# Moving an expert's output turns, and the next expert's gather, to other places between the streamed weight steps

## The chip, the cores and the metric

The kernel runs on one core of one Trainium2 chip. The metric is the device time of one launch in microseconds; the time before is the median of three runs. The rows below come from one execution that the hardware profiler recorded. Engines are named as the profile names them: PE multiplies matrices (PEld is its weight loading), DVE and ACT work elementwise, POOL is a programmable engine, SP issues the weight transfers.

## The reference, cut to what matters

Two decoder layers over 256 tokens of width 1024, all in float32. Each layer adds a mixer and a feed-forward part; the feed-forward part of the second layer is a mixture of eight experts, of which each token takes two. Only this last part is touched:

```
def moe_swiglu(h, w_router, w_gate, w_up, w_down):
    top_vals, top_idx = lax.top_k(logits, 2)       # logits = h @ w_router
    gates = jax.nn.softmax(top_vals, axis=-1)
    ...
    y_e = (silu(x_e @ w_gate[e]) * (x_e @ w_up[e])) @ w_down[e]   # x_e: tokens of expert e
    out[token] += gate * y_e[token]
```

(The last two lines stand for the reference's sort into blocks.) w_gate[e] and w_up[e] are 1024 x 3584, w_down[e] is 3584 x 1024: 44.04 MB for an expert, 352 MB for the eight, read once each.

## The kernel before, in words

**Steps.** The experts' stage is a loop over `q` from 0 to 15. `q` is half of an expert: `e, h = divmod(q, 2)`, and a half is 1792 of the 3584 hidden columns. A `q` has a gate step (`mm_in("g", q, ...)`, L984), then the down step of the half before it (`mm_down(q - 1, ...)`, L1028), then its up step (`mm_in("u", q, ...)`, L984). Called gate 5, down 4, up 5 below. `silu` (L1004, ACT) and `hidden` (L1016 and L1017, DVE) make the hidden values from the gate's and the up step's sums.

**Tokens.** An expert has room for 96 tokens in three tiles of 32. Where it has 64 or fewer, PE branches over the third tile (the `If` of `third`, branch rows L994 and L1040).

**The ring of weights.** `Stream` loads weights in the order in which the steps use them, through SP, into nine slots (`RING_A` 4 and `RING_B` 5). Of a step's weights there are four transfers: 4 x 1792 KB for a gate or up step, 2 x 2048 and 2 x 1536 KB for a down step, so 7.34 MB for any step. A slot is released when PE has read it in the first or the second half of its step (`ws.done`), and the transfer nine places later in the order is then issued (L189).

**An expert's small work.** Between the streamed steps PE does four small things for each expert:

- `fetch(e)` (L966): 16 matmuls with a one-hot matrix `G` gather the expert's tokens from `hn` into `xe`; two PSUM banks, emptied by ACT and DVE (L968).
- `prepare(e)` (L320 and L1065): transposes the one-hot matrix into `S`, and the tokens' gates into `gs`.
- `y_turn(e, n)` for n = 0, 1 (L320): four transposes each turn the expert's output `yt` back; ACT (L1083) and DVE (L1084) write it, times the gate, as two parts into `y`. `yt` comes from `y_evac` after the expert's second down step.
- `scatter(e, t, v)`, four times (L1090): two matmuls each spread `y` over the tokens, and DVE adds the result to `xt` (L1092).

All four take their PSUM from `bank("C")`, which has two banks that are handed out in turn: what comes next on a bank waits until ACT and DVE have read what stood there.

**What sets the order.** PE and SP run in the order in which the program is written (`manual_schedule`); ACT's and DVE's order is set by the framework's scheduler. Before, the small work stands at two places: `y_turn` of expert e-1 and `fetch` of expert e+1 behind up step 2e, and `scatter` of e-1 and `prepare` of e behind gate step 2e+1.

Of the kernel before, what the change touches and what calls it, by code (L numbers as in the profile page):

```python
# [20 lines left out]
E = 8  # L21
# [19 lines left out]
def hybrid_decoder(  # L41
# [20 lines left out]
    def bank(tag):  # L62
        return psum.tile([P, 512], F32, tag=tag, name=f"ps{tag}", bufs=NB[tag])
# [255 lines left out]
    def tp(dst, src, n=P):  # L319
        PE.matmul(dst, lhsT=src, rhs=ident[:n, :n], start=True, stop=True, is_transpose=True)  # L320
# [590 lines left out]
    def onehot(scol, base, tag, scale=None):  # L911
        n = base.shape[-1]
        g = moe.tile([P, 2, n], F32, tag=tag, name=tag, bufs=1)
        for t in range(2):
            if scale is None:
                DVE.tensor_scalar(g[:, t], base, scol(t), None, op0=OP.is_equal)
            else:
                DVE.tensor_scalar(g[:, t], base, scol(t), scale(t), op0=OP.is_equal, op1=OP.mult)
        return g
# [6 lines left out]
    def gates():  # L926
        r = r_ffn
        DVE.tensor_copy(gr[:, :, :, 1], r[:, :, None].to_broadcast([P, 2, E]))
        m = [sm2("m1"), sm2("m2")]
        mv = sm2("mv")  # L930
        v12 = sm(4, "v12").rearrange("p (n t) -> p n t", n=2)
        for n in range(2):
            DVE.tensor_scalar(m[n], rk, float(n), None, op0=OP.is_equal)
            DVE.tensor_tensor(mv, m[n], lg, op=OP.mult)
            DVE.tensor_reduce(v12[:, n], mv, op=OP.add, axis=AX.X)
        dv = sm(2, "dv")
        DVE.tensor_tensor(dv, v12[:, 1], v12[:, 0], op=OP.subtract)
        DVE.tensor_tensor(dv, dv, r, op=OP.mult)
        g2 = sm(2, "g2")
        ACT.activation(g2, dv, AF.Exp)  # L940
        g1 = sm(2, "g1")
        DVE.tensor_scalar(g1, g2, 1.0, None, op0=OP.add)
        DVE.reciprocal(g1, g1)
        DVE.tensor_tensor(g2, g2, g1, op=OP.mult)
        for n, g in enumerate((g1, g2)):
            DVE.tensor_tensor(m[n], m[n], g[:, :, None].to_broadcast([P, 2, E]), op=OP.mult)
        DVE.tensor_tensor(gr[:, :, :, 0], m[0], m[1], op=OP.add)
        ps = bank("C")
        PE.matmul(ps[:, 0:8], lhsT=ones, rhs=sel[:, 0], start=True, stop=False)
        PE.matmul(ps[:, 0:8], lhsT=ones, rhs=sel[:, 1], start=False, stop=True)  # L950
        cnt = sm(1, "cnt")
        DVE.tensor_reduce(cnt, ps[:, 0:8], op=OP.max, axis=AX.X)
        DVE.tensor_copy(cnt_i, cnt)
        DVE.tensor_copy(cnt_e, ps[:, 0:8])


    def fetch(e):

        g = onehot(lambda t: slot[:, t, e:e + 1], io, "G0", lambda t: r_ffn[:, t:t + 1])
        xe = moe.tile([P, KD, CAP], F32, tag="xe", name="xe")  # L960
        for n in range(2):
            ps = bank("C")[:, 0:4 * CAP].rearrange("p (j l) -> p j l", j=4)
            for j in range(4):
                c = 4 * n + j
                for t in range(2):
                    PE.matmul(ps[:, j], lhsT=hn[:, t, c * P:(c + 1) * P], rhs=g[:, t],  # L966
                              start=(j == 0 and t == 0), stop=(t == 1), skip_group_check=True)
            (DVE.tensor_copy if n else ACT.copy)(xe[:, 4 * n:4 * n + 4], ps)  # L968
        return dict(e=e, x=xe)
# [3 lines left out]
    def third(e):  # L973

        return tc.If(counts[e] > 64) if counts else ExitStack()

    def mm_in(nm, q, x):
        banks = [bank("A") for _ in range(3)]

        def tile_of(t, k0, n):  # L980
            for k in range(k0, k0 + n):
                raw = ws.direct(MU[nm, q, k - k % 2])
                for j in range(4):
                    PE.matmul(banks[t][32 * j:32 * j + 32, 0:LW], lhsT=x[:, k, 32 * t:32 * t + 32],  # L984
                              rhs=raw[:, k % 2, LW * j:LW * j + LW], start=(k == 0), stop=(k == KD - 1),
                              skip_group_check=True)

        for k0 in range(0, KD, 4):
            for k in (k0, k0 + 2):
                for t in range(2):  # L990
                    tile_of(t, k, 2)
                if k == 0:
                    tile_of(2, 0, 1)
            with third(q // 2):  # L994
                k = max(k0, 1)
                tile_of(2, k, k0 + 4 - k)
            for k in (k0, k0 + 2):
                ws.done(MU[nm, q, k])
        return banks

    def silu(bg):
        sg = big.tile([P, 3, LW], F32, tag="x0", name="sg")
        for t in range(3):
            ACT.activation(sg[:, t], bg[t][:, 0:LW], AF.Silu)  # L1004
        return sg
# [41 lines left out]
    def y_evac(psd):  # L1047

        yc = big.tile([P, 3, 256], F32, tag="x4", name="yc")
        yt = moe.tile([P, KD, CAP], F32, tag="yt", name="yt", bufs=1)  # L1050
        ACT.copy(yc[:, 0:2].rearrange("p t n -> p (t n)"), psd[0])
        ACT.copy(yc[:, 2], psd[1][:, 0:256])  # L1052
        for t in range(3):
            DVE.transpose(yt[:, :, 32 * t:32 * t + 32], yc[:, t].rearrange("p (n c) -> p n c", c=32))  # L1054
        return yt

    def prepare(st):

        e = st["e"]
        g = onehot(lambda t: slot[:, t, e:e + 1], io, "G1")  # L1060
        ps = bank("C")
        for t in range(2):
            tp(ps[0:CAP, t * P:(t + 1) * P], g[:, t])
        for t in range(2):
            PE.matmul(ps[0:CAP, T:T + 1], lhsT=g[:, t], rhs=gr[:, t, e, 0:1], start=(t == 0), stop=(t == 1),  # L1065
                      skip_group_check=True)
        s = moe.tile([P, T], F32R, tag="S", name="S", bufs=1)
        ACT.copy(s[0:CAP], ps[0:CAP, 0:T])
        gs = moe.tile([P, 1], F32, tag="gs", name="gs")
        DVE.tensor_copy(gs[0:CAP], ps[0:CAP, T:T + 1])  # L1070
        st["s"], st["gs"] = s, gs

    def y_turn(st, n):

        if n == 0:
            st["y"] = big.tile([P, 2, D], F32R, tag="x2", name="y")
        ps = bank("C")
        for b in range(4):
            tp(ps[0:CAP, b * P:(b + 1) * P], st["yt"][:, 4 * n + b])
        g = st["gs"][0:CAP]  # L1080
        q = slice(512 * n, 512 * n + 512)
        hi, lo = st["y"][0:CAP, 0, q], st["y"][0:CAP, 1, q]
        ACT.activation(hi, ps[0:CAP], AF.Copy, scale=g)  # L1083
        DVE.scalar_tensor_tensor(lo, ps[0:CAP], g, hi.bitcast(F32), op0=OP.mult, op1=OP.subtract)  # L1084

    def scatter(st, t, v):
        ps = bank("C")
        q = slice(512 * v, 512 * v + 512)
        for i in range(2):
            PE.matmul(ps, lhsT=st["s"][0:CAP, t * P:(t + 1) * P], rhs=st["y"][0:CAP, i, q],  # L1090
                      start=(i == 0), stop=(i == 1))
        DVE.tensor_tensor(xt[:, t, q], xt[:, t, q], ps, op=OP.add)  # L1092
# [3 lines left out]
    st = {0: fetch(0)}  # L1096
    psd = ht = None
    for q in range(NS):
        e, h = divmod(q, 2)
        bg = mm_in("g", q, st[e]["x"])  # L1100
        if q == 0:
            gates()
        sg = silu(bg)
        if h and e:
            for t in range(2):
                for v in range(2):
                    scatter(st[e - 1], t, v)
            st.pop(e - 1)
            prepare(st[e])
        if 0 < q < NS - 1:  # L1110
            if h:
                psd = [bank("B"), bank("B")]
            mm_down(q - 1, ht, psd)
            if not h:
                st[e - 1]["yt"] = y_evac(psd)
        bu = mm_in("u", q, st[e]["x"])
        hp, ht = ht, hidden(sg, bu, q == NS - 1)
        if h == 0:
            if e:
                for n in range(2):  # L1120
                    y_turn(st[e - 1], n)
            if e + 1 < E:
                st[e + 1] = fetch(e + 1)
            if e == 0:
                prepare(st[e])
        if q == 0:
            _, counts = nc.values_load_multi_w_load_instructions(
                cnt_e[0:1, 0:E], engines=[mybir.EngineType.PE], min_val=0, max_val=T,
                skip_runtime_bounds_check_because="a count of 256 tokens")
# [146 lines left out]
```

## Time and profile before

| | |
|---|---|
| median of three runs | 1343.11 us (1339.17 to 1346.61) |
| the profiled execution | 1340.84 us, of which the program's span is 1338.8 us |
| mean granted clock of PE | 0.984 of full speed |
| PE busy | 1224.2 us, 91% of the span |
| DVE, ACT busy | 460.2 us (34%), 267.1 us (20%) |
| HBM read | 420.74 MB, 315 GB/s over the span |

The span has two parts. Up to about 440 us run the mixers and the dense layer; from there to the end run the experts, with the router's last work at the seam. In the experts' part both the matrix engine and the transfers are busy nearly all the time, so that an average does not tell which of them sets the pace; stretches have to be looked at one by one. All times in rows are microseconds from the span's start unless marked ns.

### The profile page before, as it was taken

The numbers are of one execution on the slowest core, as the hardware profiler recorded it, in microseconds if no ns is written. First come the engines' busy times: TensorE is split into PE (matmuls) and PEld (weight loads), VectorE is DVE, ScalarE is ACT, GpSimd is POOL, SyncE is SP. The second block draws the span as 40 slices with busy tenths as digits, with TensorE's granted clock in tenths as the row PEclk, the third lists the DMA queues.
The fourth block names the chain that finished last, engine by engine and source line by source line (L and its number), as shares of the span: only waits on it lengthen the run. The fifth ranks groups of instructions, "written<-read, shape, count | busy, mean of one in ns | idle before, by whom it ended". The sixth has DMA issues, their size and how long they took to land. (4 is left out here: it accounts for less than half of the span.)

```text
span 1338.8 us, 28436 instructions
## 1 busy us (share of the span) xinstructions
PE 1224.2 (91%) x12994; PEld 775.1 (58%) x12994; DVE 460.2 (34%) x927; ACT 267.1 (20%) x446; POOL 11.9 (1%) x25
## 2 busy tenths in 40 slices
PE   4999999999999899999999999899897987887884
PEld 4997999999997644344444435434433523433342
DVE  3998765557897310102012010211211110210212
ACT  3671544445661200000000000100100000100001
POOL 3000000000000000000000000000000000000000
PEclk9999999999999899999999999999999999999997
DMA  8751565555340998998899699999999999999993
GB/s 171 277 189 63 173 237 184 174 178 175 140 173 28 381 405 338 412 410 320 361 397 416 263 423 420 407 417 416 421 421 417 422 420 416 423 419 418 419 388 135
DMA packets 91300, 423.98 MB, mean 317 GB/s; under 512 B 4590, under 2 KB 33493, under 8 KB 83476
## 3 DMA queue, kind: packets, MB, share of 16 engines
q1 hardware_dynamic: 90452, 421.09, 79.6%
q0 software_dynamic: 688, 0.72, 0.6%
q8 instruction: 122, 2.00, 0.6%
q14 instruction: 22, 0.18, 0.0%
q10 hardware_dynamic: 16, 0.00, 0.0%
HBM read 420.74 MB, written 1.05 MB: 315 GB/s over the span
## 5 line engine op out<-in xcount | busy, mean ns | idle before, releaser
L984 PE MATMUL psA<-raw,xe 128*32 128x448 f32 x5024 | 488.7, 541 | 30.2 <-DMA raw<-in_moe_w_up_dram 14.1
L984 PEld LDWEIGHTS psA<-raw,xe 128*32 128x32 f32 x5024 | 168.0, 110 | 337.5 <-issue 291.7
L1028 PE MATMUL psB<-raw,ht 128*32 128x256 f32 x4296 | 241.8, 380 | 20.3 <-DMA raw<-in_moe_w_down_dram 13.0
L1028 PEld LDWEIGHTS psB<-raw,ht 128*32 128x32 f32 x4296 | 143.3, 110 | 118.4 <-DMA raw<-in_moe_w_down_dram 23.4
L396 PE MATMUL psB<-xh,whi 128*128 128x256 f32 x608 | 173.1, 285 | 0.0
L398 PE MATMUL psB<-xh,wlo 128*128 128x256 f32 x608 | 172.5, 284 | 0.0
L397 PE MATMUL psB<-xl,whi 128*128 128x256 f32 x608 | 172.2, 283 | 0.0
L1016 DVE TENSOR_TENSOR pr<-psA,sg 128x448 f32<-128x448 f32 x48 | 43.0, 921 | 346.1 <-PE psA L984 297.3
L223 DVE TENSOR_TENSOR wlo<-raw,whi 128x1024 fp32r<-128x1024 f32 x110 | 134.2, 1224 | 59.7 <-ACT whi L222 59.6
L222 ACT CAST whi<-raw 128x1024 fp32r<-128x1024 f32 x110 | 115.0, 1050 | 113.9 <-PE psB L397 51.7
L1004 ACT ACTIVATE sg<-psA 128x448 f32<-128x448 f32 x48 | 24.5, 543 | 474.6 <-PE psA L984 464.6
L396 PEld LDWEIGHTS psB<-xh,whi 128*128 128x128 f32 x608 | 116.6, 192 | 0.7 <-issue 0.7
L397 PEld LDWEIGHTS psB<-xl,whi 128*128 128x128 f32 x608 | 116.5, 192 | 0.0
L398 PEld LDWEIGHTS psB<-xh,wlo 128*128 128x128 f32 x608 | 116.5, 192 | 0.1
L1054 DVE STREAM_TRANSPOSE yt<-yc 128x256 f32<-128x256 f32 x24 | 9.7, 431 | 245.4 <-ACT yc L1052 245.1
L680 PE MATMUL psA<-yf,raw 128*128 128x256 f32 x256 | 62.2, 399 | 5.4 <-ACT yf L720 3.0
L680 PEld LDWEIGHTS psA<-yf,raw 128*128 128x128 f32 x256 | 49.7, 199 | 13.5 <-ACT yf L720 3.5
L1092 DVE TENSOR_TENSOR xt<-xt,psC 128x512 f32<-128x512 f32 x32 | 20.8, 685 | 106.3 <-PE psC L1090 106.3
L966 PE MATMUL psC<-G,hn 128*128 128x96 f32 x256 | 36.1, 309 | 18.4 <-DVE y L1084 14.7
L527 DVE SCALAR_TENSOR_TENSOR conv<-gp,pc,conv 128x256 f32<-128x256 f32 x120 | 50.9, 480 | 0.0
L397 PE MATMUL psA<-al,whi 128*128 128x256 f32 x176 | 49.8, 283 | 0.0
L398 PE MATMUL psA<-ah,wlo 128*128 128x256 f32 x176 | 49.7, 282 | 0.0
(266 smaller groups left out, 874.5 us busy)
## 6 DMA issues: line engine op xcount, KB each, us to landing
raw<-in_moe_w_gate_dram SPq DMA_DIRECT2D x64, 1792.0 KB, 12.1
raw<-in_moe_w_up_dram SPq DMA_DIRECT2D x64, 1792.0 KB, 24.3
raw<-in_moe_w_down_dram SPq DMA_DIRECT2D x30, 2048.0 KB
raw<-in_moe_w_down_dram SPq DMA_DIRECT2D x30, 1536.0 KB, 17.6
raw<-in_w_in_dram SPq DMA_DIRECT2D x9, 2048.0 KB, 14.0
raw<-in_ffn_w_gate_dram SPq DMA_DIRECT2D x11, 1024.0 KB, 5.6
raw<-in_ffn_w_up_dram SPq DMA_DIRECT2D x11, 1024.0 KB, 8.1
raw<-in_ffn_w_down_dram SPq DMA_DIRECT2D x5, 2048.0 KB, 9.1
```

The costliest lines, as they stand in the source:

```text
L222: ACT.copy(hi, raw)
L223: DVE.tensor_tensor(lo, raw, hi.bitcast(F32), op=OP.subtract)
L396: PE.matmul(ps, lhsT=hi, rhs=xh, start=start, stop=False, **kw)
L397: PE.matmul(ps, lhsT=hi, rhs=xl, start=False, stop=False, **kw)
L398: PE.matmul(ps, lhsT=lo, rhs=xh, start=False, stop=stop, **kw)
L527: DVE.scalar_tensor_tensor(conv[:, c], src, w, conv[:, c], op0=OP.mult, op1=OP.add)
L680: PE.matmul(acc[j][:, a], lhsT=raw[:, k, w], rhs=yf[b][:, k], start=(b + k == 0 and a == 0), stop=(b + k == 4), skip_group_check=True)
L966: PE.matmul(ps[:, j], lhsT=hn[:, t, c * P:(c + 1) * P], rhs=g[:, t], start=(j == 0 and t == 0), stop=(t == 1), skip_group_check=True)
L984: PE.matmul(banks[t][32 * j:32 * j + 32, 0:LW], lhsT=x[:, k, 32 * t:32 * t + 32], rhs=raw[:, k % 2, LW * j:LW * j + LW], start=(k == 0), s ...
L1004: ACT.activation(sg[:, t], bg[t][:, 0:LW], AF.Silu)
L1016: DVE.tensor_tensor(pr[:, t], by(bu[t][:, 0:LW]), by(sg[:, t]), op=OP.mult)
L1028: PE.matmul(psd[t // 2][32 * j:32 * j + 32, 256 * (t % 2):256 * (t % 2) + 256], lhsT=ht[:, t, b], rhs=w[:, j], start=(h == 0 and b == 0 an ...
```

## The change

`y_turn` goes from behind up step 2e to behind gate step 2e+1, ahead of down step 2e. `fetch`, `scatter` and `prepare` go behind that down step, in this order, ahead of up step 2e+1. For q = 15, where no down step stands between gate and up, `y_turn`, `scatter` and `prepare` follow each other directly. `prepare(0)` and `fetch(1)` move from q = 0 to q = 1 in the same way. No instruction is added or removed.

```diff
         sg = silu(bg)
         if h and e:
-            for t in range(2):
-                for v in range(2):
-                    scatter(st[e - 1], t, v)
-            st.pop(e - 1)
-            prepare(st[e])
+            for n in range(2):
+                y_turn(st[e - 1], n)
         if 0 < q < NS - 1:
             if h:
                 psd = [bank("B"), bank("B")]
             mm_down(q - 1, ht, psd)
             if not h:
                 st[e - 1]["yt"] = y_evac(psd)
+        if h:
+            if e + 1 < E:
+                st[e + 1] = fetch(e + 1)
+            if e:
+                for t in range(2):
+                    for v in range(2):
+                        scatter(st[e - 1], t, v)
+                st.pop(e - 1)
+            prepare(st[e])
         bu = mm_in("u", q, st[e]["x"])
         hp, ht = ht, hidden(sg, bu, q == NS - 1)
-        if h == 0:
-            if e:
-                for n in range(2):
-                    y_turn(st[e - 1], n)
-            if e + 1 < E:
-                st[e + 1] = fetch(e + 1)
-            if e == 0:
-                prepare(st[e])
```

PE's order around the second turn (`y_turn` of expert 1; `G_6890` is the one-hot matrix of the gather for expert 3, `G_7043` that of `prepare(2)`), before:

```order
L320 MATMUL psC<-ident,yt 96x128 x8
L966 MATMUL psC<-G_6890,hn 128x96 x16
L984 MATMUL psA<-raw,xe 32x448 x36
L994 COMPARE_AND_BRANCH
L984 MATMUL psA<-raw,xe 32x448 x12
L994 UNCONDITIONAL_BRANCH x2
L984 MATMUL psA<-raw,xe 32x448 x32
L994 COMPARE_AND_BRANCH
L984 MATMUL psA<-raw,xe 32x448 x16
L994 UNCONDITIONAL_BRANCH x2
L1090 MATMUL psC<-y,S 128x512 x8
L320 MATMUL psC<-ident,G_7043 96x128 x2
```

The same place after (`G_7183` and `G_7223` are the same two matrices under other numbers):

```order
L320 MATMUL psC<-ident,yt 96x128 x8
L1028 MATMUL psB<-raw,ht 32x256 x68
L1040 COMPARE_AND_BRANCH
L1028 MATMUL psB<-raw,ht 32x256 x28
L1040 UNCONDITIONAL_BRANCH x2
L1028 MATMUL psB<-raw,ht 32x256 x48
L1040 COMPARE_AND_BRANCH
L1028 MATMUL psB<-raw,ht 32x256 x24
L1040 UNCONDITIONAL_BRANCH x2
L966 MATMUL psC<-G_7183,hn 128x96 x16
L1090 MATMUL psC<-y,S 128x512 x8
L320 MATMUL psC<-ident,G_7223 96x128 x2
```

Between the transposes and the next use of the C banks there now stands a whole down step, and gather, scatter and `prepare` follow each other without a streamed step between them.

DVE's order at this place, before:

```order
L1016 TENSOR_TENSOR pr<-psA,sg 128x448 x2
L1017 STREAM_TRANSPOSE ht<-pr 128x448 x2
L1084 SCALAR_TENSOR_TENSOR y<-psC,gs,y 96x512 x2
L968 COPY xe<-psC 128x384
L918 TENSOR_SCALAR G_7782<-io,slot,rstd 128x96 x2
L994 UNCONDITIONAL_BRANCH x2
L1092 TENSOR_TENSOR xt<-xt,psC 128x512 x4
L916 TENSOR_SCALAR G_7935<-io,slot 128x96 x2
L1070 COPY gs<-psC 96x1
```

And after:

```order
L1016 TENSOR_TENSOR pr<-psA,sg 128x448 x2
L1017 STREAM_TRANSPOSE ht<-pr 128x448 x2
L994 UNCONDITIONAL_BRANCH x2
L1084 SCALAR_TENSOR_TENSOR y<-psC,gs,y 96x512 x2
L1040 UNCONDITIONAL_BRANCH x2
L968 COPY xe<-psC 128x384
L1092 TENSOR_TENSOR xt<-xt,psC 128x512 x4
L918 TENSOR_SCALAR G_8075<-io,slot,rstd 128x96
L1070 COPY gs<-psC 96x1
L918 TENSOR_SCALAR G_8075<-io,slot,rstd 128x96
L916 TENSOR_SCALAR G_8115<-io,slot 128x96 x2
```

The two writes of `y` (L1084) stood directly behind the products and transposes of `hidden`, and now a gate step later; the four sums into `xt` (L1092) now stand directly behind the copy of the gathered tokens (L968).

PE's order at the last odd step, q = 15, before (then the rest of gate 15, and the scatter behind it):

```order
L320 MATMUL psC<-ident,yt 96x128 x8
L984 MATMUL psA<-raw,xe 32x448 x36
L994 COMPARE_AND_BRANCH
L984 MATMUL psA<-raw,xe 32x448 x12
L994 UNCONDITIONAL_BRANCH x2
```

And after:

```order
L320 MATMUL psC<-ident,yt 96x128 x8
L1090 MATMUL psC<-y,S 128x512 x8
L320 MATMUL psC<-ident,G_11482 96x128 x2
L1065 MATMUL psC<-gr,G_11482 96x1 x2
L984 MATMUL psA<-raw,xe 32x448 x36
```

Here nothing stands between the transposes and the scatter any more.

## Rows read from the trace of the kernel before

**Rows 1.** Who waited: PE's waits from 430 us on (total us, times, longest).

```profile
PE psC L966 <- DVE y L1084: 14.7, 6, 2.6
PE psA L984 <- DMA raw<-in_moe_w_up_dram: 14.1, 13, 2.3
PE psB L1028 <- DMA raw<-in_moe_w_down_dram: 13.0, 12, 1.7
PE psA L984 <- DMA raw<-in_moe_w_gate_dram: 11.1, 11, 1.7
```

**Rows 2.** Stretches: window, PE, PEld, DVE, ACT, POOL busy (instructions), PE clock, DMA share, GB/s.

```profile
620.00:660.00 40.00, 39.51 (x546) 18.92 (x542) 3.13 (x7) 1.89 (x4) 0.00 (x0) 1.00 0.79 309
...
740.00:770.00 30.00, 29.50 (x402) 14.07 (x398) 3.13 (x7) 1.89 (x4) 0.00 (x0) 1.00 0.72 275
770.00:840.00 70.00, 68.91 (x912) 33.09 (x904) 8.65 (x13) 3.18 (x7) 0.00 (x0) 1.00 1.02 421
840.00:880.00 40.00, 35.77 (x420) 19.31 (x421) 6.82 (x15) 2.83 (x6) 0.00 (x0) 0.96 0.99 404
880.00:1280.00 400.00, 347.90 (x4050) 154.77 (x4049) 59.96 (x101) 23.58 (x47) 0.00 (x0) 0.99 1.01 420
```

**Rows 3.** PE in order of time, around the first turn (start, us, what, idle before).

```profile
608.24 1.08 PE L320 MATMUL psC<-ident,yt 128*96 128x128 f32 x8
611.90 3.81 PE L966 MATMUL psC<-G,hn 128*128 128x96 f32 x32 [2.58 <-DVE y L1084]
615.64 18.25 PE L984 MATMUL psA<-raw,xe 128*32 128x448 f32 x192
633.82 1.20 PE L1090 MATMUL psC<-y,S 96*128 96x512 f32 x4
635.33 1.33 PE L1090 MATMUL psC<-y,S 96*128 96x512 f32 x4 [0.32 <-DVE xt L1092]
636.83 0.42 PE L320 MATMUL psC<-ident,G 128*96 128x128 f32 x2 [0.17 <-DVE xt L1092]
...
637.44 18.34 PE L1028 MATMUL psB<-raw,ht 128*32 128x256 f32 x336
```

**Rows 4.** DVE in order of time, at the first turn.

```profile
610.05 1.16 DVE L1017 STREAM_TRANSPOSE ht<-pr 128x448 f32<-128x448 f32 x2
611.14 1.36 DVE L1084 SCALAR_TENSOR_TENSOR y<-psC,gs,y 96x512 fp32r<-96x512 f32 x2
615.75 0.56 DVE L968 COPY xe<-psC 128x384 f32<-128x384 f32 x1 [3.25 <-PE psC L966]
```

**Rows 5.** PE in order of time, the gathers of the second and third turn.

```profile
731.62 3.81 PE L966 MATMUL psC<-G,hn 128*128 128x96 f32 x32 [2.58 <-DVE y L1084]
...
842.06 5.44 PE L966 MATMUL psC<-G,hn 128*128 128x96 f32 x32 [2.46 <-DVE y L1084]
```

**Rows 6.** The stretch of the third gather, columns as in rows 2.

```profile
842.00:847.50 5.50, 5.44 (x36) 5.35 (x40) 0.66 (x2) 0.48 (x1) 0.00 (x0) 0.69 0.99 417
```

**Rows 7.** SP's issues of weight transfers, four of them (start, us to the last one, what).

```profile
766.08 0.37 SPq L189 DMA_DIRECT2D raw<-in_moe_w_gate_dram  x1
...
800.47 0.89 SPq L189 DMA_DIRECT2D raw<-in_moe_w_up_dram  x2
...
854.55 0.89 SPq L189 DMA_DIRECT2D raw<-in_moe_w_up_dram  x2
...
872.28 6.37 SPq L189 DMA_DIRECT2D raw<-in_moe_w_gate_dram  x3
```

**Rows 8.** PE in order of time, the last down steps and the last turn.

```profile
1285.62 4.09 PE L1028 MATMUL psB<-raw,ht 128*32 128x256 f32 x72 [1.69 <-DMA raw<-in_moe_w_down_dram]
...
1290.56 3.66 PE L1028 MATMUL psB<-raw,ht 128*32 128x256 f32 x64 [0.85 <-DMA raw<-in_moe_w_down_dram]
...
1321.62 4.14 PE L1090 MATMUL psC<-y,S 96*128 96x512 f32 x8 [1.17 <-DVE y L1084]
```

## The prediction

> **What bounds the kernel now.** I read PE's waits first, then the stretches, then PE's order of time around a turn, then SP's issues. Of PE's waits in the experts' part the longest line is the one this change is about: the gather waits for DVE's writes of `y`, 14.7 us in six turns [rows 1]. The next three lines are waits for weights, 14.1 + 13.0 + 11.1 = 38.2 us [rows 1]: somewhere PE is ahead and the transfers set the pace. The stretches say where. From 880 to 1280 us the transfers run at a share of 1.01 and 420 GB/s, and PE is busy 347.9 of 400 us; from 620 to 660 and from 740 to 770 us it is the reverse, PE busy 39.51 of 40 and 29.50 of 30 us and the transfers at 0.79 and 0.72 [rows 2]. The reader is to see two regimes. In the first, of experts 0 to 2, which use the third tile (192 records in a gate step, [rows 3]), PE takes 731.62 - 611.90 = 119.7 us for an expert [rows 3, 5], while its six steps of 7.34 MB take 6 x 17.5 = 104.9 us at 420 GB/s: PE sets the pace, the nine slots are full, and transfers stop until PE releases one. In the second, transfers never stop, and a PE wait removed there is waited for again at the next weight.
>
> So the end is set thus: a transfer issued at time t with B bytes still to come cannot let the stream end before t + B / 420 GB/s, and the issue for which that sum is largest decides. I call it the issue's end. Four issues matter [rows 7]; between two of them I compare the time passed with the steps' bytes (17.48 us a step). 766.08 (released by down 4, it ends the hole seen in 740 to 770) is the first. 800.47 (released by gate 6) comes 34.39 us and two steps later: 34.39 - 34.95 = -0.56, its end is 0.56 us earlier. 854.55 (by gate 7): 54.08 us, three steps: +1.65. 872.28 (by down 6): 17.73 us, one step: +0.25. So 872.28 decides before, 1.34 us above 766.08 and 1.90 us above 800.47. That the transfers did lose something there shows in 840 to 880 us: 404 GB/s against 421 and 420 beside it [rows 2]; 40 x (1 - 404/420) = 1.5 us.
>
> **The change part by part.** Nothing is added or removed; sums go against the profiled execution, 1340.84 us, 2.3 us under the median of 1343.11.
>
> *The wait behind the transposes.* Before, a gather wants the two C banks that the transposes filled, and DVE empties them last: behind the rest of `hidden` (until 610.05 + 1.16) and two writes of 1.36 us [rows 4]. PE idles 2.58 us in each of the first two turns and 2.46 in the third [rows 3, 5]. After, a down step of 18 us [rows 3] stands there and hides the writes. Nobody is queued behind them who is in a hurry: the banks' next user is 18 us away, and the up step needs only the gate's products, which ACT makes ahead of `y`. Taken: the whole 2.58 us.
>
> *A new wait behind the gather.* The second scatter takes the bank that DVE's copy of `xe` empties: 0.56 us, beginning 0.11 us after PE could go on at 615.64 [rows 3, 4]. The first scatter covers half of 1.20 us [rows 3], so 0.56 + 0.11 - 0.60 = 0.07 us shows, and the sums into `xt`, already waited for with 0.32 and 0.17 us [rows 3], may stand one such delay later. Bounds: 0, since the gather's copy could be covered wholly, and 0.56, the whole copy. I take 0.15, near the lower, because the rows put the copy beside the scatter. Net 2.58 - 0.15 = 2.43 us a turn.
>
> *Places.* Per odd step PE reaches the gate 615.64 - 608.24 = 7.40 us earlier than its old place in the sequence, and the down step another 3.62 (633.82 to 637.44) less the transposes' 1.0 earlier: 10.0 us; the gathered block of 3.74 + 3.62 us then stands ahead of the up step, which gains only the 2.43 [rows 3]. Slots that gate and down hold are released that much sooner, those of the up step only by what was saved. No transfer is issued by the moved work itself; SP's order stays, and POOL has nothing here.
>
> *Sum.* Two turns lie ahead of gate 6, so 800.47 moves by 2 x 2.43 = 4.86 us. 766.08, released by a down step, moves by 2.43 + 10.0 = 12.4; 854.55 by 4.86 + 7.4 and 872.28 by 4.86 + 10.0 at least. After the change 800.47 decides. The stream ends 1.90 + 4.86 = **6.8 us** earlier: about 4.9 us of PE waiting, and 1.9 us of holes that the new places no longer make. Behind it the transfers have no reason to stop: a block of 7.4 us against nine slots of 4.4 us each. The later three turns' waits are beside transfers and give nothing.
>
> *The clock.* The third gather took 5.44 instead of 3.81 us: the granted clock is 0.69 over it [rows 6], so it was at the lower of its two levels, 1.2 GHz, for part, after PE had idled 2.46 us. These 1.63 us lie between 800.47 and 854.55. In an execution without that fall 854.55 and 872.28 come down by 1.63, below 766.08, which then decides: the gain is 4.86 + 0.56 = 5.4 us. A fall in one of the first two turns, which the profile does not have, would make it about 8.4. So 5.4 to 8.4, and 0.8 less with the new wait at its upper bound: 4.6 to 8.4.
>
> *The last turn.* At q = 15 the scatter follows the transposes directly. The kernel's end has this sequence already and waits 1.17 us in it [rows 8]; with ACT's silu ahead it may be the 2.58 of the first turn [rows 3]. With the transposes' own 1.0 us, up 15 starts 2.2 to 3.6 us later against its weights. Behind it PE waits for weights anyway, 1.69 and 0.85 us in the next two rows [rows 8] and more later; I charge 0, with 0 to 1 us as its bounds.
>
> Profiled execution: 1340.84 - 6.8 = 1334.0. Median: 1343.11 - 6.8 = **1336.3 us**.
>
> **The rivals.**
>
> *Hidden anyway: 1343.1 us.* The transfers bound the whole part, and PE's waits are beside them. For it: 1.01 over 400 us [rows 2]. Against it: 0.79 and 0.72 in the stretches of the first turns. By the Trainium skill (Perfetto Trace Analysis, Identifying the Most-Contended Engine) the engine with the highest occupancy is to be worked on first, for transfers judged by bandwidth; by that rule, over the part as a whole, no time would change. The same page (Optimization Strategy) allows for regimes whose bound changes, and the trace agrees with that: 309 and 275 GB/s there, 420 later. Chance 0.14.
>
> *All six waits come off the end: 1343.1 - 14.7 = 1328.4 us.* It holds if PE still sets the pace in the later turns. Against it: the 38.2 us of waits for weights [rows 1], and 1.01 from 880 on. For it: the smaller holes of 840 to 880 show that the third turn still counts. Chance 0.09.
>
> *The clock falls in the gathered block: 1357 us.* Gather, scatter and `prepare` are small matmuls, 7.4 us in a row now, with sums of DVE in between. If PE's clock went to its lower level there and stayed through half of the next up step (9.1 us), in the three blocks ahead of gate 6, then at the gather's ratio (1.63 / 3.81 = 43%) it costs 3 x 16.5 x 0.43 = 21 us against the 6.8: 1343.1 - 6.8 + 21 = 1357. It makes the kernel slower by half a per cent from 13.5 us on, that is 4.5 us in each of the three blocks. For it: the one fall at 842 is in a gather [rows 6]. Against it: that fall came after PE had idled, which the change takes away, and scatter and `prepare` ran at 1.00 from 620 to 660 [rows 2]. By the Trainium skill (TensorE: Matmul & The Clock Gate, What's actually happening) the gate follows how busy PE has just been; the trace agrees in that the fall stands behind an idle stretch. Chance 0.07.
>
> **How the numbers follow.** Forecast 0.70, hidden 0.14, all six 0.09, clock 0.07. What a measurement can tell from no change is about 0.5%, 6.7 us, and the forecast lies at this bound. With a fall of the clock in one of the first turns possible on one side and its absence in the third on the other, I put 0.55 of the forecast beyond it: faster 0.70 x 0.55 + 0.09 = 0.48, same 0.70 x 0.45 + 0.14 = 0.45, slower 0.07. The forecast's own range is 1343.1 less 4.6 to 8.4 and the scatter of the runs, 1332 to 1341; to hold 8 in 10 it reaches most of the hidden case above and part of the six waits below: 1330 to 1344.
>
> **What would show it.** Right: no wait of L966 for `y`; PE without idle time between transposes and down step; up 5 begins about 4.9 us earlier, gate 5 and down 4 some 10 and 12 us; in each of the first experts one hole of 8 to 12 us, behind the down step of the odd half, instead of two; no hole after gate 6; the span near 1332 us; the waits for weights longer than 38 us. Wrong: transfers below 400 GB/s after 820 us, a wait of scatter above 0.6 us in the blocks, a clock below 1.00 in them, or an up 15 that pushes the last down steps back.

## The result, and the profile after

The changed kernel takes 1334.13 us (median of six, 1329.68 to 1335.07), the kernel before, timed beside it, 1342.20 us (1339.17 to 1347.20). The ratio is 0.9923, with a 95% interval of 0.9900 to 0.9946: 10.3 us faster, 7.2 to 13.4. The ratio is not the quotient of the two medians, which lie 8.1 us apart; where the two differ below, both are given. A second comparison (e10 below) gave 0.9923 again, 0.9896 to 0.9950. The forecast was 1336.3 us, a gain of 6.8.

The profiled execution took 1329.68 us; its span is 1327.7 us, 11.1 under the span before. First the page's busy row, granted clock and DMA share, each slice being a fortieth of the span.

```profile
PE 1213.8 (91%) x12994; PEld 765.2 (58%) x12994; DVE 460.5 (35%) x927; ACT 265.8 (20%) x446; POOL 11.9 (1%) x25
...
PEclk9999999999999999999999999999999999999997
DMA  8751565544440999999899989999999999999993
```

PE is as busy as before, 91%. The granted clock has no slice below 9 but the last; the page of the kernel before has an 8 in its fourteenth slice, 435 to 469 us, which comes back below. Averages say nothing here, as before. The waits do (total us, times, longest), to be set against [rows 1]:

```profile
PE psB L1028 <- DMA raw<-in_moe_w_down_dram: 19.9, 20, 1.7
PE psA L984 <- DMA raw<-in_moe_w_gate_dram: 19.2, 19, 1.4
PE psA L984 <- DMA raw<-in_moe_w_up_dram: 14.3, 12, 2.0
...
PE psC L1090 <- DVE xe L968: 0.8, 5, 0.2
PE psC L1090 <- DVE xt L1092: 0.6, 4, 0.2
```

The gather's 14.7 us for `y` are gone. The three waits for weights are longer, 53.4 us instead of 38.2: in total PE waits as long for weights and `y` together as before (52.9 us then). The first turn, which answers to [rows 3], reads now (PE in order of time: start, us, what, idle before):

```profile
621.68 1.08 PE L320 MATMUL psC<-ident,yt 128*96 128x128 f32 x8
622.68 18.34 PE L1028 MATMUL psB<-raw,ht 128*32 128x256 f32 x336
640.95 3.81 PE L966 MATMUL psC<-G,hn 128*128 128x96 f32 x32
644.55 0.71 PE L1090 MATMUL psC<-y,S 96*128 96x512 f32 x2
645.41 1.36 PE L1090 MATMUL psC<-y,S 96*128 96x512 f32 x4 [0.15 <-DVE xe L968]
646.93 0.74 PE L1090 MATMUL psC<-y,S 96*128 96x512 f32 x2 [0.16 <-DVE xt L1092]
...
648.16 2.09 PE L984 MATMUL psA<-raw,xe 128*32 128x448 f32 x20
```

Transposes and down step follow each other without idle time, and the gather starts with none. DVE shows why: it writes `y` at 623.39, 0.7 us into the down step, and empties the gather's bank at 644.80.

```profile
623.39 1.41 DVE L1084 SCALAR_TENSOR_TENSOR y<-psC,gs,y 96x512 fp32r<-96x512 f32 x2 [16.78 <-ACT y L1083]
...
644.80 0.56 DVE L968 COPY xe<-psC 128x384 f32<-128x384 f32 x1 [20.00 <-PE psC L966]
```

The stretches, as in [rows 2] (the last two rows are the one place of the first and of the second turn where transfers nearly stop):

```profile
620.00:660.00 40.00, 39.69 (x538) 21.52 (x534) 5.58 (x12) 2.97 (x6) 0.00 (x0) 1.00 0.85 337
740.00:770.00 30.00, 29.71 (x434) 17.61 (x426) 5.60 (x12) 1.70 (x4) 0.00 (x0) 1.00 0.92 369
...
840.00:880.00 40.00, 38.47 (x466) 20.24 (x462) 9.20 (x17) 3.51 (x7) 0.00 (x0) 1.00 1.02 420
880.00:1260.00 380.00, 319.19 (x3793) 139.69 (x3782) 55.84 (x95) 22.74 (x46) 0.00 (x0) 1.00 1.01 419
...
650.00:660.00 10.00, 10.00 (x112) 3.51 (x108) 0.00 (x0) 0.00 (x0) 0.00 (x0) 1.00 0.47 179
768.00:774.00 6.00, 6.00 (x68) 2.08 (x64) 0.00 (x0) 0.00 (x0) 0.00 (x0) 1.00 0.16 44
```

PE is still what sets the pace in the first two turns, but transfers lose less there (337 and 369 GB/s against 309 and 275), and from 840 us on nothing: 420 against 404.

**What of the 11.1 us is the change's.** The two executions reach gate step 0 at different times, ahead of everything that was moved. PE in order of time in the trace of the kernel before, a row of the layer ahead of the experts and the begin of gate 0:

```profile
432.42 5.41 PE L680 MATMUL psA<-yf,raw 128*128 128x256 f32 x16 [1.52 <-ACT yf L720]
...
458.57 7.72 PE L984 MATMUL psA<-raw,xe 128*32 128x448 f32 x80
```

and in the trace of the changed kernel, with SP's issue that decides there:

```profile
430.25 3.72 PE L680 MATMUL psA<-yf,raw 128*128 128x256 f32 x16 [1.52 <-ACT yf L720]
...
453.96 6.22 PE L984 MATMUL psA<-raw,xe 128*32 128x448 f32 x64
...
790.26 0.93 SPq L189 DMA_DIRECT2D raw<-in_moe_w_up_dram  x2
```

Gate 0 comes 4.6 us earlier in the one profile. Over the thirteen traces of this study it lies anywhere from 453.2 to 458.6 us, for one and the same kernel at 453.96 and 455.48, so most of it is chance: the first gather took 6.16 us in the one and 5.41 in the other, and from 100 to 200 us the granted clock is 0.98 and 1.00. Not all of it is: the row of L680 above takes 5.41 us in all five traces of kernels that have only the old places (before, e11, e1, e5, e9) and 3.72 us in all eight that have new ones, behind the same idle time of 1.52 us. The granted clock over it is 0.68 before and 1.00 after. These 1.7 us come with the change in every trace, though its edit does not touch that part; why is not shown. Issues are counted from gate 0 here, and the prediction's "issue's end" too, at 421 GB/s, the rate of a stretch where transfers don't stop [rows 2].

| issue | before | after | moved | forecast |
|---|---|---|---|---|
| 766.08, by down 4 | 307.5 | 294.5 | 13.0 | 12.4 |
| 800.47, by gate 6 | 341.9 | 336.3 | 5.6 | 4.86 |
| 854.55, by gate 7 | 396.0 | 381.6 | 14.3 | at least 12.3 |
| 872.28, by down 6 | 413.7 | 396.7 | 17.0 | at least 14.9 |
| latest end | 845.2 | 837.5 | 7.7 | 6.8 |

Before, 872.28 has the latest end; after, the counterpart of 800.47, as forecast. Two further traces put the ends at 845.24 and 837.54, within 0.02 us of the first two. What follows the latest end is 35.0 us before and 36.2 after, in the repeated pair 37.9 and 36.8: no difference that has one sign. From gate 0 to the end of the span the gain is so 6.5 us in the first pair and 8.7 in the repeated one. The latest end is a bound from the four issues, not the landing itself: by the traces' transfer records the last weights are in 858.6 us from gate 0 before and 852.1 after, 859.0 and 851.9 in the repeated pair. That is 6.5 and 7.1 us, on both sides of the forecast's 6.8.

### The profile page after: what moved, and what is told of

Same layout as the page of the kernel before. It is cut to its first block, busy times and chain, and to the rows that moved or that the text cites. A ratio compares the mean times of both kernels' runs of the same rounds, so it can differ in the third digit from the quotient of the medians.

```text
span 1327.7 us, 28435 instructions
## 1 busy us (share of the span) xinstructions
PE 1213.8 (91%) x12994; PEld 765.2 (58%) x12994; DVE 460.5 (35%) x927; ACT 265.8 (20%) x446; POOL 11.9 (1%) x25
## 5 line engine op out<-in xcount | busy, mean ns | idle before, releaser
L680 PE MATMUL psA<-yf,raw 128*128 128x256 f32 x256 | 58.8, 383 | 5.4 <-ACT yf L720 3.0
L968 DVE COPY xe<-psC 128x384 f32<-128x384 f32 x8 | 4.5, 558 | 152.8 <-PE psC L966 152.8
L680 PEld LDWEIGHTS psA<-yf,raw 128*128 128x128 f32 x256 | 47.4, 190 | 12.5 <-ACT yf L720 3.5
L1084 DVE SCALAR_TENSOR_TENSOR y<-psC,gs,y 96x512 fp32r<-96x512 f32 x16 | 11.2, 742 | 110.6 <-ACT y L1083 110.6
```

Source lines behind the costliest of these rows:

```text
L680: PE.matmul(acc[j][:, a], lhsT=raw[:, k, w], rhs=yf[b][:, k], start=(b + k == 0 and a == 0), stop=(b + k == 4), skip_group_check=True)
```

## The experiments

The theory: a wait of the gather counts in the first two turns, where the slots are full, and not in the last three; the third counts partly; it is the wait that counts, and the places add the holes. The rivals: all six waits count, or what moved in the sequence and not the wait made the gain. Where a trace can decide, the latest end from gate 0 is given, 845.2 before and 837.5 after.

**e1: the wait alone.** The kernel before, with the gather put ahead of the transposes in its old place.

```diff
         if h == 0:
+            if e + 1 < E:
+                st[e + 1] = fetch(e + 1)
             if e:
                 for n in range(2):
                     y_turn(st[e - 1], n)
-            if e + 1 < E:
-                st[e + 1] = fetch(e + 1)
```

> The kernel before with one thing exchanged: the gather of expert e+1 stands ahead of the transposes of expert e-1 behind the even up step, all other places as before. Theory (the wait on the two C banks counts, in the first two turns): the gather finds its banks empty, the transposes wait at most a few tenths for the copy of the gathered tokens, and DVE's writes of y are hidden behind the gate step, so PE saves about 2.5 us a turn; the issue near 766 us then decides, 2 x 2.5 us earlier, and 1.3 us of the hole behind it goes too if the clock fell there before: 5 to 6.5 us faster than before, ratio 0.995 to 0.996. Rival (the places of the streamed steps matter, not the wait): the places are nearly those of before, so 0 to 1 us.

Measured: 1334.46 us, ratio 0.9939 (0.9916 to 0.9961), 8.2 us, more than the 5 to 6.5 that were expected, and 5.9 by the medians (1340.40 for the kernel before). PE in order of time in e1's first turn:

```profile
605.76 3.81 PE L966 MATMUL psC<-G,hn 128*128 128x96 f32 x32
609.41 0.60 PE L320 MATMUL psC<-ident,yt 128*96 128x128 f32 x4
610.23 0.64 PE L320 MATMUL psC<-ident,yt 128*96 128x128 f32 x4 [0.21 <-DVE xe L968]
```

The gather waits for nothing and the transposes 0.21 us for its copy. The end is at 838.9, 6.3 us earlier. So most of the gain needs no other place in the program, only another order on the two banks; what the change's places add over this is 1.4 us by the latest ends, and 2.7 by the last landing (854.8 here).

**e2: the places with half of the wait.** The changed kernel, with the transposes behind the down step, directly ahead of the gather.

```diff
-        if h and e:
-            for n in range(2):
-                y_turn(st[e - 1], n)
         ...
         if h:
+            if e:
+                for n in range(2):
+                    y_turn(st[e - 1], n)
             if e + 1 < E:
                 st[e + 1] = fetch(e + 1)
```

> The changed kernel with the transposes put behind the down step as well, so that transposes, gather, scatter and prepare follow each other: the new places, but with the wait between transposes and gather back, without hidden's work ahead of it on DVE. Theory: PE waits 1.2 to 1.3 us before each gather, as in the kernel's own last turn, so a turn saves 1.5 instead of 2.8 us; 2 x 1.3 us of the gain goes: 2.6 us slower than the changed kernel, ratio to before about 0.994 to 0.995. Rival (places alone): as the changed kernel, 0.992.

Measured: 1334.57 us, ratio 0.9944 (0.9922 to 0.9966). PE in order of time, the same place in e2's first turn:

```profile
641.66 1.08 PE L320 MATMUL psC<-ident,yt 128*96 128x128 f32 x8
...
643.86 3.81 PE L966 MATMUL psC<-G,hn 128*128 128x96 f32 x32 [1.12 <-DVE y L1084]
```

Without `hidden` ahead of it DVE is sooner done, and the wait is 1.12 us and not 2.58. Two of them ahead of gate 6 are 2.24 us, and the end is at 839.6, 2.1 later than with the change. The wait comes back one for one where it should; the same waits in the later turns leave nothing.

**e3 and e4: the change for the early experts alone, and for the late ones alone.**

```diff
+        new = e < 3
         if h and e:
-            for n in range(2):
-                y_turn(st[e - 1], n)
+            if new:
+                for n in range(2):
+                    y_turn(st[e - 1], n)
+            else:
...
-        if h:
+        if h and new:
...
+        if h == 0 and not new:
...
```

What the left-out lines hold are the old places, `scatter` and `prepare` in the first, `y_turn` and `fetch` in the last. In e4 `new` is `e > 2`.

> The change for experts 0 to 2 alone (turns of experts 0 and 1, gates 3 and 5); the later five turns stand as before. Theory (only where PE sets the pace does its wait count): about 5.6 us for the two turns, less the holes of 840 to 880, which stay: 5 to 6 us faster than before, ratio 0.9955 to 0.9965. Rival (all waits come off the end): a third of the six, 5 us, so this run alone tells nothing; with the next one it does.

> The change for experts 3 to 7 alone (the last five turns); the first two turns stand as before. Theory: the transfers run without a stop from 880 us on, so their waits are waited for again at the weights: 0 to 1.9 us faster than before (the holes of 840 to 880), ratio 0.9985 to 1.000. Rival (all six waits come off the end): four waits of 2.5 us, 10 us faster, ratio 0.9925.

Measured: e3 1333.82 us, ratio 0.9943 (0.9922 to 0.9964), a little more than was expected; e4 1341.49 us, ratio 1.0011 (0.9989 to 1.0033). In e3 four waits of 9.7 us remain, and its end is at 839.6, now set by the counterpart of 872.28, behind the third turn: two turns give 5.6 us, the third decides over the rest. e4 has removed the late waits, in its trace two are left (PE's waits, total us, times, longest):

```profile
PE psC L966 <- DVE y L1084: 5.2, 2, 2.6
```

and no time went with them. That all six waits come off the end is out: the late ones gave less than 1.5 us (the lower end of e4's interval). In e4's trace the first turn reads, and its gather's stretch (columns as in [rows 2]):

```profile
603.01 1.08 PE L320 MATMUL psC<-ident,yt 128*96 128x128 f32 x8
...
606.67 6.75 PE L966 MATMUL psC<-G,hn 128*128 128x96 f32 x32 [2.58 <-DVE y L1084]
...
606.00:613.40 7.40, 6.73 (x36) 6.64 (x40) 1.27 (x2) 0.48 (x1) 0.00 (x0) 0.54 0.94 387
```

The gather took 6.75 instead of 3.81 us at a granted clock of 0.54, next to its lower level of 1.2 GHz, and the second turn's 6.85. The prediction had named such a fall as possible and not seen one. Two of them, 2.94 + 3.04 = 6.0 us, lie ahead of gate 6 in this execution, and its latest end is at 849.6, 4.4 us later than before; less the 6.0 it would be 843.6, 1.6 us earlier, which is an estimate. Hence the next experiment.

**e5: the idle time filled.** The kernel before, with eight of the kernel's own `keep_warm` matmuls between transposes and gather, for the first two turns only. Their results are not used.

```diff
                 for n in range(2):
                     y_turn(st[e - 1], n)
+            if e in (1, 2):
+                keep_warm(8)
```

> The kernel before with eight matmuls of 128x128 (about 2.1 us) put between the transposes and the gather of the first two turns: the wait of 2.58 us stays, but PE is busy in it. Theory (part of the measured gain is the clock, which falls behind that idle time in some executions and makes the gather 6.8 instead of 3.8 us): no gather of the first two turns is longer than 3.9 us, the slow executions of before (1342 to 1347 us) do not occur, and the median is 1 to 2 us lower, ratio 0.9985 to 0.9995. Rival (the clock's falls there are chance and not bound to the wait): spread and median as before, ratio 1.000, and some gather near 6.8 us.

Measured: 1339.63 us (12 runs) against 1341.46 (28 runs), ratio 0.9977 (0.9957 to 0.9997): 3.1 us, 0.4 to 5.8, and 1.8 by the medians. PE in order of time in its first turn:

```profile
607.41 1.08 PE L320 MATMUL psC<-ident,yt 128*96 128x128 f32 x8
608.33 1.95 PE L326 MATMUL psA<-ones 128*128 128x128 f32 x16
611.09 3.81 PE L966 MATMUL psC<-G,hn 128*128 128x96 f32 x32 [0.81 <-DVE y L1084]
```

The gather starts no sooner: 611.09 lies 153.35 us after this trace's gate 0, 611.90 before 153.33. So the 3.1 us are not waiting. Both filled gathers take 3.81 us, the four that are not filled 5.44. That alone says little of the first two turns, where both traces of the kernel before have 3.81 without filling, and only e4's has two falls. The timed runs say more. Of the 28 of the kernel before 16 lie above 1341 us, of e4, which keeps the two waits, 8 of 12, and of e5 none of 12: its longest is 1340.31, as the theory had it and the rival not. The mean granted clock of the runs, recorded for each, is on average 0.9825 before and 0.9848 in e5. A fall like e4's, 7.4 us at 0.54, takes 7.4 x 0.46 / 1340 = 0.0025 off it, so that the difference is about one such fall in an execution, some 3 us; this is an estimate, since no trace shows where the timed runs' falls lie.

**e6 and e7: work put in early, and late.** The changed kernel with eleven more matmuls, as those of the gather, in the gathers of experts 2 and 3 (e6, `e in (2, 3)`) or 5 to 7 (e7, `e > 4`). They are written over by what follows, and so add work alone.

```diff
+            for _ in range(11 if n == 0 and e in (2, 3) else 0):
+                PE.matmul(ps[:, 0], lhsT=hn[:, 0, 0:P], rhs=g[:, 0], ...)
```

> The changed kernel with eleven more matmuls of 128x96 (2.6 us) in the gathers of experts 2 and 3, where PE sets the pace. Their results are written over. Theory: each costs its full 2.6 us, as the wait that the change removed did: 5.2 us slower than the changed kernel, ratio to before about 0.998. Rival (all is beside transfers): no difference to the changed kernel, 0.994.

> The same eleven matmuls in the gathers of experts 5, 6 and 7, where the transfers set the pace: 3 x 2.6 = 7.9 us of PE work. Theory: no difference to the changed kernel, ratio to before 0.993 to 0.995, and the waits for weights about 8 us shorter. Rival (PE's time counts everywhere): 7.9 us slower, 0.999.

Measured: e6 1336.45 us, ratio 0.9972 (0.9951 to 0.9994); e7 1332.81 us, ratio 0.9935 (0.9915 to 0.9954), beside the same runs of the kernel before. PE's begin of gate 0 and SP's deciding issue in e6:

```profile
454.07 6.22 PE L987 MATMUL psA<-raw,xe 128*32 128x448 f32 x64
...
795.27 0.89 SPq L189 DMA_DIRECT2D raw<-in_moe_w_up_dram  x2
```

795.27 - 454.07 = 341.2, against 336.3 for the change: 22 matmuls early came out as 4.9 us. The same two rows in e7, and its waits for weights:

```profile
453.19 7.34 PE L987 MATMUL psA<-raw,xe 128*32 128x448 f32 x75
...
789.48 0.89 SPq L189 DMA_DIRECT2D raw<-in_moe_w_up_dram  x2
...
PE psB L1031 <- DMA raw<-in_moe_w_down_dram: 18.7, 20, 1.8
...
PE psA L987 <- DMA raw<-in_moe_w_gate_dram: 13.8, 14, 1.3
PE psA L987 <- DMA raw<-in_moe_w_up_dram: 13.3, 12, 2.1
```

The issue stays at 336.3, and 33 matmuls, 33 x 4.9 / 22 = 7.4 us of work, came out of the waits for weights: 45.8 us instead of 53.4. PE's time is worth one for one in the first turns and nothing in the last ones, shown here with work added, as e3 and e4 show it with waits removed.

**e8 and e9: the experts in another order.** If PE sets the pace in experts 0 to 2 and the transfers in 3 to 7, the ring could carry the one over the other if they took turns. e8 is the changed kernel with the experts computed in the order 3, 0, 4, 1, 5, 2, 6, 7; e9 is the kernel before with the same order.

```diff
+    TURN = [3, 0, 4, 1, 5, 2, 6, 7]
-        e, h = divmod(q, 2)
+        e, h = TURN[q // 2], q % 2
...
```

The line on `e, h` stands in the order of both kinds of weights; one-hots, gates and counts take `TURN[e]` for `e`.

> The changed kernel with the experts in another order, 3 0 4 1 5 2 6 7: the three experts whose third tile runs (119 us of PE against 105 us of transfers) each stand between two whose third tile is left out (95 us of PE). The sum over experts is the same. Theory (the transfers lose time only while full slots meet an expert slower than the stream; after a short expert the slots are empty and take up the 15 us by which a long one lags): nearly all holes between 500 and 870 us go, some 20 to 27 us off the changed kernel, ratio to before 0.975 to 0.980. Rival (the total of PE's work is what holds it): no change, 0.994.

> The kernel before (old places, wait of 2.5 us in every turn) with the experts in the order 3 0 4 1 5 2 6 7, to lie beside the run with the new places in that order. Theory (in this order transfers hardly stop, so a wait of PE has nothing to set): the new places bring 0 to 2 us here instead of the 7 to 8 they bring in the old order: ratio to before 0.9755 to 0.978. Rival (the wait and the clock's falls cost PE time that counts in any order): 7 to 10 us behind the other, ratio 0.981 to 0.983.

Measured: e8 1308.49 us (1306.60 to 1309.91), ratio 0.9755 (0.9721 to 0.9790); e9 1315.37 us, ratio 0.9782 (0.9755 to 0.9810), in another comparison. The stretches of e8, columns as in [rows 2]:

```profile
500.00:620.00 120.00, 117.74 (x1522) 59.67 (x1518) 13.02 (x23) 7.41 (x15) 0.00 (x0) 1.00 1.01 419
620.00:740.00 120.00, 117.64 (x1460) 59.76 (x1456) 19.77 (x37) 6.73 (x14) 0.00 (x0) 1.00 1.01 417
740.00:870.00 130.00, 128.22 (x1554) 57.71 (x1550) 20.03 (x33) 5.89 (x12) 0.00 (x0) 1.00 1.01 421
870.00:1240.00 370.00, 343.77 (x4262) 161.10 (x4255) 55.86 (x94) 22.71 (x46) 0.00 (x0) 1.00 1.01 419
```

There are no holes between 500 and 870 us any more, and PE is 98% busy up to there: both resources are used up together. This is the fastest kernel of the study, 2.4% under the kernel before. The Trainium skill (Perfetto Trace Analysis, Optimization Strategy) says that performance may be improved by interleaving regimes when the most-contended engine changes over time; here the order alone, in e9, was worth 2.2%, where the change was worth 0.8%. The order fits this input, in which three experts have over 64 tokens; another routing would want another one.

e9 was expected to lie 2 us behind e8 at most. By ratios it is 3.6 us behind, with intervals that overlap, by medians 6.9, so that the timed runs leave it open. The two traces do not: from gate 0 (457.35 and 456.41) to the end of the span it is 850.7 us in e8 and 859.8 in e9, 9.1 us more, which is the rival's size. Its waits and stretches:

```profile
PE psC L968 <- DVE y L1086: 15.1, 6, 2.6
...
PE psB L1030 <- DMA raw<-in_moe_w_down_dram: 3.5, 4, 1.7
...
500.00:620.00 120.00, 114.80 (x1330) 56.55 (x1323) 14.57 (x24) 7.16 (x14) 0.00 (x0) 0.97 0.99 406
620.00:740.00 120.00, 115.45 (x1564) 58.86 (x1563) 16.41 (x31) 6.37 (x13) 0.00 (x0) 1.00 1.00 412
740.00:870.00 130.00, 124.61 (x1494) 57.94 (x1498) 17.05 (x29) 6.00 (x12) 0.00 (x0) 0.99 0.99 406
```

With PE and transfers level, PE waits little for weights, and the transfers are slower in every stretch (406 to 412 GB/s). I had expected the ring to hide the waits for `y`, as it does late in the old order, and overlooked that the new order uses up the slack that hid them. The waits are not alone in this: four of the six gathers behind them fell to the lower clock (7.06, 5.44, 5.44 and 7.07 us), 9.8 us together beside the 15.1 of waits. What share of the 9.1 us each has was not tried.

**e10 and e11: both kernels again.**

> The changed kernel once more, beside the others on one chip. Theory: 6 to 8 us faster than before (two turns of 2.8 us, 0.6 to 1.9 us of holes), and some 1 to 3 us more on average for the clock's falls in the removed waits: ratio 0.993 to 0.995, and no record of a clock at the lower level from gate 0 to the last down step where PE sets the pace.

> The kernel before once more, for its trace: whether the clock falls in the waits of the first two turns. Theory: the gather behind a wait is 3.8 us without a fall, 5.4 to 6.8 us with one, and the execution's time follows, about 3 us for each fall in the first two turns; falls in later turns move nothing. Rival: falls and times are not connected.

Measured: e10 1332.72 us (1331.46 to 1335.27), ratio 0.9923 (0.9896 to 0.9950); e11, one execution, 1343.23 us. Their latest ends are the 837.54 and 845.24 given above. e11's trace has no fall in the first two turns and takes 1343.23 us all the same: gate 0 is as late as before, and 37.9 us follow the latest end instead of 35.0. A fall is in that, too, in another place: the last 96 records of the last down step take 7.07 us at a clock of 0.76, in the profile before 5.70 at 1.00. So a long execution does not need falls in the early turns, but the rival, that falls and times are not connected, is out: of the 28 runs of the kernel before beside e5, the 13 above 1342 us have a mean granted clock of 0.977 to 0.982, the 15 below it 0.982 to 0.986.

## Why the prediction was right, point by point

**What bounds: right.** Two regimes, and the latest issue decides. All four issues moved by the forecast and 0.6 to 2.1 us more; before 872.28 decided and after 800.47's counterpart; each of e1, e2, e3 and e6 moved the latest end as its edit says, e7 left it alone, and e4 comes to 1.6 us once its two falls are taken out. The name of the second term was wrong, though. The forecast put 1.9 us to holes that the new places no longer make. In e1, which has the old places, the counterpart of 872.28 comes 8.6 us earlier all the same (three waits of 7.6 us and the third gather's fall of 1.6, less 0.6 of new waits) and lies at 836.6, below e1's latest end. So what held 872.28 up was the third turn's wait and fall. The places bring the 1.4 us by which the change lies ahead of e1. The last weights' landing, 6.5 and 7.1 us earlier, was as near to the forecast as the bound, 7.7; and the forecast did not have the 1.7 us ahead of gate 0.

**The wait: right, a little small.** 2.43 us a turn were forecast, 5.6 / 2 = 2.80 measured. The term that was mis-sized is the new wait. It is there, 0.8 us in five blocks, 0.15 a block as taken. But the waits for `xt` that stood in the old block, 0.32 + 0.17 [rows 3], shrank to 0.6 us in four: the whole gathered block takes 648.16 - 640.95 = 7.21 us, where its two parts took 3.74 + 3.62 = 7.36. I had charged 0.15 for the block, and it gained 0.15. The wait itself was worth more than its 2.58 us, too: from the begin of the transposes to the begin of what follows them it was 611.90 - 608.24 = 3.66 us and is 622.68 - 621.68 = 1.00, since the down step begins before the transposes' record ends. 2.66 + 0.15 = 2.81 us.

**The holes that the places leave: right in number, too large.** There is no hole after gate 6 (420 GB/s), and early slots come free 13 to 17 us sooner, as forecast. The one hole behind the down step of each early odd half instead of two is there as well, but smaller than the 8 to 12 us: 10 x (1 - 179/421) = 5.7 us in the first turn and 6 x (1 - 44/421) = 5.4 in the second. Before, the first turn had two, the first of them in this stretch (columns as in [rows 2]):

```profile
616.00:626.00 10.00, 10.00 (x112) 3.51 (x108) 0.78 (x3) 0.00 (x0) 0.00 (x0) 1.00 0.35 105
```

It is 7.5 us by the same sum, and the other 5.2 (642 to 650 us, 147 GB/s). I had counted the hole from the time without an issue and left out that the issues before it were still landing. That changed nothing in the sum, which goes by issues.

**The clock: right in kind, wrong in weight.** The third turn's fall was charged rightly: the profile after has none in any turn, and in 840 to 880 the clock is 1.00. But "a fall in one of the first two turns, which the profile does not have" was left at the edge of the range, when the third turn's fall had come after the very same idle time. e4 shows two at 2.94 and 3.04 us, and e5 their average worth, 3.1 us (0.4 to 5.8), or 1.8 by medians. Whether they make up the sum is not shown. From gate 0 the traces' latest ends, free of such falls, give 7.7 us, the timed runs 10.3 by ratio and 8.1 by medians. For e1 the three are 6.3, 8.2 and 5.9, for e2 5.6, 7.5 and 5.8, for e3 5.6, 7.6 and 6.6. By ratio there are 2 to 3 us over each time, by medians at most 1; the intervals hold both, and e1, e2 and e3 share one set of runs of the kernel before. The 1.7 us ahead of gate 0 belong in this sum as well, for the change, e2 and e3. What speaks for the falls is that e5 has no long executions.

**The last turn: right.** The scatter waits 1.31 us there, and the down steps behind it still wait for weights (the changed kernel, PE in order of time):

```profile
1257.25 2.90 PE L1090 MATMUL psC<-y,S 96*128 96x512 f32 x8 [1.31 <-DVE y L1084]
...
1275.39 0.85 PE L1028 MATMUL psB<-raw,ht 128*32 128x256 f32 x12 [1.12 <-DMA raw<-in_moe_w_down_dram]
```

**The rivals.** Hidden anyway fell with e3 (0.9943) and the result. All six fell with e4 and e7. The clock did not fall in the gathered block: the early blocks ran at 1.00 (620 to 660 us, above). The Trainium skill (TensorE: Matmul & The Clock Gate, What's actually happening) states that the gate follows how busy PE has been recently. The traces agree with that here: of the gathers behind a wait of 2.2 to 2.6 us for `y`, 16 of 28 took 5.44 to 7.07 us, and of the twelve behind the moved turns in the two traces of the changed kernel none was longer than 3.81.

**The chances.** 0.45 for "same" looks too much now, though one outcome does not show that. The forecast lay at the 0.5% bound, and the one known cost that the profile happened not to show, falls in the early turns, lay wholly on the side of faster.

## What to carry to other kernels

A wait on the compute engine is worth its time only where its buffers are full: find the issue after which the stream never stops, and count the waits ahead of it. Work that takes turns on the same few banks should stand apart, with a long step between, or in the order in which the banks come free soonest (e1 has most of the gain with two blocks exchanged). Where two resources bind in different stretches, first try to mix the stretches (e8), and then count the waits anew, since fewer of them are hidden (e9).

## What the runs showed of the hardware

Idle time of 2.2 to 2.6 us ahead of the gather was followed by the lower clock in 16 of 28 turns (in none of the first two of the kernel before in its two traces, in both of e4's), and for unequal times: the same 32 records (16 matmuls) took 3.81, 5.44, 6.75, 6.85, 7.06 and 7.07 us. Behind 1.12 us (e2) one of six took 5.44. The first gather of the stage, behind 3.7 us, took 5.41 to 7.04 us in all thirteen traces. With 1.95 us of matmuls in the idle time both filled gathers took 3.81, and the executions above 1341 us were gone. And the front, which the edits leave alone, takes 453.2 to 458.6 us up to gate 0, a spread of more than half of what the change is worth, with 1.7 us that go with the kernel; two spans can't be compared here without taking it out.
